# Loading x through GpSimd's DMA queue with a cast to f16, in place of SyncE's queue and casts on ScalarE

One core of one Trainium2 chip. The metric is the device time of one execution in microseconds (us), the median of several. The medians are of all runs of a kernel.

## The reference

```python
def setup_inputs():
    batch, m, k, n = 16, 512, 1024, 768      # all float32
    return {"x": randn(batch, m, k), "weight": randn(k, n), "sub_value": randn(batch, m, n)}

def reference(x, weight, sub_value):
    return (np.matmul(x, weight) - sub_value).astype(np.float32)
```

8192 rows of x in 64 row tiles of 128; 33.55 MB of x and 3.15 MB of weight are read, 25.17 MB of sub_value read and 25.17 MB of output written.

## The kernel before

Every transfer is issued by SyncE, one after another, in a sequence set by hand (x, w = weight, s = sub_value, o = output; first tile or chunk, number). x lands as f32 in 16 slots; sub_value and output share 32 slots, and each subtraction is done in place. ScalarE casts a tile of x to f16; TensorE transposes it (f16 pairs taken as f32) into PSUM, where TensorE's results go; ScalarE copies it out; 16 matmuls follow; VectorE subtracts. Seven pairs of tiles are transposed by VectorE instead.

```python
NX, NSO = 16, 32
TRANSFERS = [
    ('x', 0, 1), ('w', 0, 1), ('x', 1, 1), ('w', 1, 1), ('x', 2, 1), ('w', 2, 1),
    ('w', 3, 1), ('x', 3, 2), ('s', 0, 1), ('x', 5, 3), ('s', 1, 3), ('x', 8, 3),
    ('s', 4, 4), ('x', 11, 5), ('s', 8, 8), ('x', 16, 8), ('x', 24, 3), ('s', 16, 8),
    ('x', 27, 5), ('o', 0, 8), ('s', 24, 8), ('x', 32, 8), ('s', 32, 8), ('o', 8, 8),
    ('x', 40, 8), ('s', 40, 8), ('x', 48, 8), ('o', 16, 8), ('o', 24, 8), ('s', 48, 8),
    ('x', 56, 8), ('s', 56, 8), ('o', 32, 8), ('o', 40, 8), ('o', 48, 8), ('o', 56, 4),
    ('o', 60, 2), ('o', 62, 1), ('o', 63, 1),
]
# ... issue(): issues from the head of the list, and stops where the entry's buffer isn't free yet
#   ('x': the tile NX before has been cast, 's': the tile NSO before has been stored, 'o': subtracted)
def cast(mi):
    ...
    keep(nc.scalar.copy(out=x16_t[mi], in_=x_ring[:, mi % NX]))   # f16 <- f32
    issue()
# ... main loop, per tile: matmuls(mi), between them the transposes of tile mi + 2; cast of tile mi + 4
def finish(mi):
    o = so_ring[:, mi % NSO].rearrange("p (h n) -> p h n", h=2)
    keep(nc.vector.tensor_tensor(out=o, in0=po_t.pop(mi)[:, :, :NS], in1=o, op=subtract))
    issue()
```

## Time and profile before

| | before |
|---|---|
| time, median | 211.16 us (210.99 to 211.29) |
| span of the profiled run | 209.4 us |
| TensorE busy | 198.4 us, 95% |
| DMA engines busy (queue 1) | 97.7%, 87 MB |
| ScalarE busy | 112.6 us, 54% |

Two resources are full at once, so anything that makes either of them stand still for a while is paid for in full. The lines and how to read them are in the prediction.

### The profile page before, as it was taken

The page shows a single profiled execution, that of the slowest core. Times are in us where ns is not written, and L with a number is a line of the kernel's source. Part 1 is how long each engine was busy: PE and PEld are TensorE (multiplying, and loading weights), DVE is VectorE, ACT ScalarE, POOL GpSimd, SP SyncE. Part 2 cuts the span into 40 slices and gives each one's busy share as a digit, 9 for nine tenths or more (in the row PEclk, how much of TensorE's full clock was granted, in tenths as well). Part 3 has the DMA queues.
Part 4 walks back from the last instruction along what each step waited for, and adds up shares of the span by engine and source line. Part 5 has one row for each costly group of instructions (what it writes and reads, how often), then busy time and mean ns, then how long its engine had stood idle before and what let it go on. Part 6 is the DMA issues. An engine that isn't in the chain of part 4 may idle for free.

```text
span 209.4 us, 2967 instructions
## 1 busy us (share of the span) xinstructions
PE 198.4 (95%) x1249; PEld 130.4 (62%) x1249; DVE 114.1 (54%) x186; ACT 112.6 (54%) x115; POOL 0.7 (0%) x6
## 2 busy tenths in 40 slices
PE   7998789999979999999999999999999999999990
PEld 2464467676656576676666666667666766766660
DVE  0342044206149849929946965992994795332231
ACT  3555565675396183655727629355573760765410
POOL 1000000000000000000000000000000000000000
PEclk9999999999999999999999999999999999999999
DMA  6999999999999999999999999999999999999994
GB/s 221 420 426 424 424 438 439 433 443 426 391 455 415 442 427 423 454 413 432 435 421 449 423 413 444 451 418 421 418 441 440 423 437 418 426 446 427 415 383 167
DMA packets 5629, 87.22 MB, mean 417 GB/s; under 512 B 624, under 2 KB 624, under 8 KB 2032
## 3 DMA queue, kind: packets, MB, share of 16 engines
q1 hardware_dynamic: 5616, 87.03, 97.7%
q8 instruction: 10, 0.16, 0.3%
q14 instruction: 3, 0.02, 0.0%
HBM read 61.87 MB, written 25.17 MB: 416 GB/s over the span
## 4 chain that ended last, share of the span: by engine, by line
PE 68%; DMA 20%; ACT 4%; DVE 3%; SPq 1%; issue 1%
PE psum_o L177 60%; DMA x_ring<-in_x_dram 20%; PE psum_t L144 8%; ACT x_tile L135 2%; DVE xtp_tile L165 2%; ACT xt_tile L151 1%; DVE so_ring L189 1%; SPq L110 1%; SPq L122 1%; ACT x16p_tile L132 0%
## 5 line engine op out<-in xcount | busy, mean ns | idle before, releaser
L177 PE MATMUL psum_o<-w_sb,xt_tile 128*128 128x384 f16 x800 | 145.7, 326 | 1.7 <-ACT xt_tile L151 1.1
L177 PEld LDWEIGHTS <-xt_tile 128*128 128x128 f16 x800 | 78.2, 98 | 41.5 <-ACT xt_tile L151 1.9
L189 DVE TENSOR_TENSOR so_ring<-psum_o,so_ring 128x768 f32<-128x768 f32 x64 | 60.7, 957 | 61.2 <-PE psum_o L177 41.1
L151 ACT COPY xt_tile<-psum_t 128x1024 f16<-128x1024 f16 x50 | 50.6, 1012 | 75.7 <-PE psum_t L144 74.9
L165 DVE STREAM_TRANSPOSE xtp_tile<-x16p_tile 32x256 f32<-32x256 f32 x112 | 48.8, 436 | 18.9 <-ACT x16p_tile L132 17.2
L144 PE MATMUL psum_t<-ident,x_tile 128*128 128x128 f32 x200 | 52.5, 275 | 2.8 <-ACT x_tile L135 2.4
L135 ACT CAST x_tile<-x_ring 128x1024 f16<-128x1024 f32 x50 | 51.6, 1049 | 5.5 <-DMA x_ring<-in_x_dram 5.5
L177 PE MATMUL psum_o<-w_sb,xtp_tile 128*128 128x384 f16 x224 | 42.9, 326 | 0.3 <-DVE xtp_tile L165 0.3
L144 PEld LDWEIGHTS psum_t<-ident,x_tile 128*128 128x128 f32 x200 | 27.8, 142 | 16.8 <-ACT x_tile L135 4.7
L177 PEld LDWEIGHTS <-xtp_tile 128*128 128x128 f16 x224 | 21.8, 98 | 10.4 <-DVE xtp_tile L165 0.7
L132 ACT CAST x16p_tile<-x_ring 128x1024 f16<-128x1024 f32 x14 | 14.6, 1046 | 5.8 <-DMA x_ring<-in_x_dram 4.7
L205 PE MATMUL psum_o<-idle_x,idle_w 128*128 128x512 f16 x25 | 8.8, 508 | 1.3 <-DVE idle_x L200 1.3
L112 DVE CAST w_sb<-so_ring 128x768 f16<-128x768 f32 x8 | 4.1, 556 | 10.5 <-DMA so_ring<-in_weight_dram 10.5
L205 PEld LDWEIGHTS <-idle_w 128*128 128x128 f16 x25 | 3.0, 120 | 5.0 <-issue 3.2
L135 ACT ACT_TABLE_LOAD x1 | 1.3, 1283 | 0.7 <-PEq L277 0.7
L199 DVE MEMSET idle_w<- 128x64 uint32 x1 | 0.1, 112 | 0.8 <-PEq L277 0.8
masks.py:199 POOL TENSOR_SCALAR_AFFINE_SELECT ident<-ident 128x128 f32<-128x128 f32 x1 | 0.3, 292 | 0.1
L200 DVE MEMSET idle_x<- 128x256 uint32 x1 | 0.3, 272 | 0.0
masks.py:197 POOL MEMSET ident<- 128x128 f32 x1 | 0.2, 205 | 0.3 <-POOLq L277 0.3
L277 POOL MEMSET const-bfloat16-1.0<- 128x1 bf16 x1 | 0.1, 101 | 0.0
L277 POOL MEMSET const-uint8-127<- 128x1 uint8 x1 | 0.1, 101 | 0.0
L277 POOL MEMSET const-float32-0.0<- 128x1 f32 x1 | 0.1, 98 | 0.2 <-issue 0.2
(1 smaller groups left out, 0.1 us busy)
## 6 DMA issues: line engine op xcount, KB each, us to landing
so_ring<-in_sub_value_dram SPq DMA_DIRECT2D x7, 3072.0 KB, 24.2
out_dram<-so_ring SPq DMA_DIRECT2D x7, 3072.0 KB, 31.2
x_ring<-in_x_dram SPq DMA_DIRECT2D x5, 4096.0 KB, 22.3
x_ring<-in_x_dram SPq DMA_DIRECT2D x2, 2560.0 KB, 23.3
x_ring<-in_x_dram SPq DMA_DIRECT2D x3, 1536.0 KB, 19.8
so_ring<-in_weight_dram SPq DMA_DIRECT2D x4, 768.0 KB, 8.7
x_ring<-in_x_dram SPq DMA_DIRECT2D x3, 512.0 KB, 6.2
so_ring<-in_sub_value_dram SPq DMA_DIRECT2D x1, 1536.0 KB, 22.2
```

The costliest lines, as they stand in the source:

```text
L110: keep(nc.sync.dma_start(out=st, in_=w_c[at]))
L112: keep(nc.vector.tensor_copy(out=w_sb[:, at, r], in_=st[:, r]))
L122: keep(nc.sync.dma_start(out=here, in_=there))
L132: keep(nc.scalar.copy(out=x16_t["pair", first][:, mi - first], in_=x_in))
L135: keep(nc.scalar.copy(out=x16_t[mi], in_=x_in))
L144: keep(nc.tensor.transpose(ps_t[mi].bitcast(F32)[:, c * P : (c + 1) * P], x16_t[mi].bitcast(F32)[:, c * P : (c + 1) * P], ident,))
L151: keep(nc.scalar.copy(out=xt_t[mi], in_=ps_t.pop(mi)))
L165: keep(nc.vector.transpose(xt[b * Q : (b + 1) * Q, :, a * Q : (a + 1) * Q], x16[a * Q : (a + 1) * Q, :, b * Q : (b + 1) * Q],))
L177: keep(nc.tensor.matmul(po_t[mi][:, h, :NS], xt_t[mi][:, 2 * P * c + r : 2 * P * (c + 1) : 2], w_sb[:, c, r, h * NS : (h + 1) * NS], start ...
L189: keep(nc.vector.tensor_tensor(out=o, in0=po_t.pop(mi)[:, :, :NS], in1=o, op=mybir.AluOpType.subtract))
L205: keep(nc.tensor.matmul(idle_o[:, 0], idle_w, idle_x, start=True, stop=True))
L277: nc = _bacc.Bacc("TRN2", target_bir_lowering=False, num_devices=1)
```

## The change

Intent: take the 64 casts (67 us) off ScalarE, halve the room of x in SBUF so that 32 slots fit where 16 did, and feed the transposes straight from the ring. The loads of x, which now cast, are issued by GpSimd, so x gets a list of its own:

```diff
-NX, NSO = 16, 32
+NX, NSO = 32, 32
-TRANSFERS = [ ... one sequence, above ... ]
+TRANSFERS = {"pool": [
+    ('x', 0, 1), ('x', 1, 1), ('x', 2, 1), ('x', 3, 1), ('x', 4, 4), ('x', 8, 8),
+    ('x', 16, 8), ('x', 24, 8), ('x', 32, 8), ('x', 40, 8), ('x', 48, 8), ('x', 56, 8),
+], "sp": [
+    ('w', 0, 1), ('w', 1, 1), ('w', 2, 1), ('w', 3, 1), ('s', 0, 4), ('s', 4, 4),
+    ('s', 8, 8), ('o', 0, 8), ('s', 16, 8), ('o', 8, 8), ('s', 24, 8), ('o', 16, 8),
+    ('s', 32, 8), ('o', 24, 8), ('s', 40, 8), ('o', 32, 8), ('s', 48, 8), ('o', 40, 8),
+    ('s', 56, 8), ('o', 48, 8), ('o', 56, 4), ('o', 60, 2), ('o', 62, 1), ('o', 63, 1),
+]}
-    x_ring = x_pool.tile([P, NX, K], F32)
+    x_ring = x_pool.tile([P, NX, K], F16)
-            if kind == "o":
+            if kind == "x":
+                keep(nc.gpsimd.dma_start(out=here, in_=there))
+            elif kind == "o":
-    def cast(mi): ...                        # and its calls
-                    x16_t[mi].bitcast(F32)[:, c * P : (c + 1) * P],
+                    x_ring[:, mi % NX].bitcast(F32)[:, c * P : (c + 1) * P],
```

## The prediction

> **What bounds the kernel now.** I read the page first: totals, then the 40 slices.
>
> ```profile
> span 209.4 us, 2967 instructions
> PE 198.4 (95%) x1249; PEld 130.4 (62%) x1249; DVE 114.1 (54%) x186; ACT 112.6 (54%) x115; POOL 0.7 (0%) x6
> ...
> DMA  6999999999999999999999999999999999999994
> GB/s 221 420 426 424 424 438 439 433 443 426 391 455 415 442 427 423 454 413 432 435 421 449 423 413 444 451 418 421 418 441 440 423 437 418 426 446 427 415 383 167
> ...
> q1 hardware_dynamic: 5616, 87.03, 97.7%
> ```
>
> Two things are full, not one. TensorE is busy for 95% of the span and the DMA engines for 97.7%, from the second slice to the last but one. ScalarE, whose casts the change removes, is busy for 54%. The stretches give the same by stage:
>
> ```profile
> 20.00:30.00 10.00, 7.95 (x52) 5.06 (x50) 3.36 (x4) 5.88 (x7) 0.00 (x0) 1.00 1.01 422
> ...
> 40.00:60.00 20.00, 18.78 (x123) 12.70 (x121) 4.74 (x6) 12.52 (x14) 0.00 (x0) 1.00 1.01 430
> 60.00:80.00 20.00, 19.66 (x129) 13.07 (x127) 15.64 (x28) 11.89 (x13) 0.00 (x0) 1.00 0.99 425
> 80.00:100.00 20.00, 20.00 (x131) 13.48 (x130) 15.27 (x28) 10.73 (x11) 0.00 (x0) 1.00 1.01 432
> ```
>
> (Stretch, its length, busy time of PE, PEld, DVE, ACT, POOL with instruction counts, granted clock, DMA share, GB/s.) From 80 us on TensorE never rests, and the DMA is full beside it. Where the two stand to each other in the steady state: a block of 8 row tiles moves 4.19 MB of x, 3.15 MB of sub_value and 3.15 MB of output, 10.49 MB, at 430 GB/s 24.4 us. TensorE takes some 3.04 us for a tile that it transposes itself (16 matmuls in four groups of 0.65 us, four transposes of 0.11 us in the chain) and 2.6 us for one of the pair that VectorE transposes: a block of six and two takes 23.4 us. So the DMA is, by 1 us in 24, the slower of the two, and only its lead hides it. This kernel has nothing left over to repay a late start of the work.
>
> The timeline of TensorE shows when the pipeline is under way:
>
> ```profile
> 33.02 0.81 PE L177 MATMUL psum_o<-w_sb,xt_tile 128*128 128x384 f16 x4
> 33.67 0.27 PE L144 MATMUL psum_t<-ident,x_tile 128*128 128x128 f32 x1
> ```
>
> Counting four groups per tile back from the first matmul of tile 3 at 21.57, this is tile 6, with the first transpose of tile 8 after its first group. From 33.67 to the last matmul at 204.5 are 170.8 us, with TensorE idle for 1.5 of them (1.2 in 40 to 60, 0.3 in 60 to 80). The last subtraction, the last store and its semaphore take the 4.9 us from 204.5 to the end.
>
> **What the Trainium skill says.** "DMA: Bandwidth & Descriptors", section "SWDGE vs HWDGE vs iDMA": a cast in a DMA has to be issued from GpSimd, whose cores write the descriptors in software; its packets are preferably up to 4096 bytes. No run here has one yet. The same page, "Queues, rings and completion order": each DMA engine goes round-robin between queues that have work, by packet. The trace has one working queue, so doesn't test it, but 39 transfers of 128 rows and 16 completions are 39 x 144 = 5616, the packet count of q1: a hardware packet is a whole row here, 4 to 32 KB. The same page, "Where 436 GB/s comes from", puts the ceiling at the SBUF ports, 435 GB/s. The trace agrees in size (424 in 44 to 54, loads alone; 430 in 154 to 194, when only stores are issued). It also shows that loads and stores together get no more (432 in 80 to 100), so the shared limit looks like the engine's own data path, not the side that writes SBUF. "SBUF — State Buffer", section "Who interferes with whom": VectorE in a two-port mode blocks GpSimd from writing descriptors. The subtraction takes 957 ns for 768 elements, about one per 0.96 GHz cycle, so no doubled mode; only the eight weight casts (556 ns for the same 768) could do it, 4.4 us in all, at the start.
>
> **The change, part by part.**
>
> Removed: 64 casts on ScalarE, 50 x 1049 ns and 14 x 1046 ns, 67 us, which makes ScalarE's busy time about 52. Little of it is on the path:
>
> ```profile
> PEld psum_t L144 <- ACT x_tile L135: 4.7, 5, 1.8
> ...
> PE psum_t L144 <- ACT x_tile L135: 2.4, 2, 1.4
> ```
>
> TensorE and its weight loads waited for casts for 2.4 and 4.7 us, overlapping each other, and those waits end in x landing just before. I allow 1 us per tile for tiles 0 to 4, and nothing later. It is swallowed below, because data come later than that. The instructions of TensorE and VectorE keep their number, order and shape: the listing of the changed kernel differs only in line numbers and in the source tile. So TensorE needs the same 170.8 - 1.5 = 169.3 us from tile 8's first transpose to the end of its work.
>
> Not saved: DMA time. x is still 33.55 MB of f32 read from HBM. It writes half as many bytes, but since loads and stores share one limit I take a load to cost what its wider side costs. Total 87 MB at 430 GB/s, 202 us, as before.
>
> Moved, and this decides: the order. Before, one queue held a hand-made sequence: what precedes the landing of x tiles 8 to 10 is x 0 to 10 (5.77 MB), the weights (3.15) and s 0 to 3 (1.57), 10.5 MB; at 430 GB/s 24.4 us, with 2 us before the first byte 26.4, well before 33.67. After, x 8 to 15 is one transfer with one completion, and SyncE's queue has the weights and s 0 to 15 outstanding with no wait between. What moves before tile 8 is released is then x 0 to 15 (8.39), weights (3.15) and s 0 to 15 (6.29): 17.8 MB, 41.5 us, plus 2 us for the start and 1 for completion: 44.5. This hardly depends on how the packets are shared. At equal shares x's 8.39 MB take 39 us at 215 GB/s plus the 4 us of start and completion; with packets of 4 KB against rows of 6, 12 and 24 KB, s wins (SyncE's 9.4 MB done at about 32) and x 8 to 15 comes last, at the same 44. In the second case tile 4 (in a transfer of four) is late too, about 35 instead of 18, but that lies inside the same delay.
>
> So tile 8's transpose starts at 44.5 instead of 33.67, 10.8 us late. TensorE ends at 44.5 + 169.3 = 213.8, the span is 213.8 + 4.9 = 218.7, and the time adds the 1.8 us by which 211.19 exceeds 209.4: 220.5.
>
> A second term is the sharing later on. x may now run 32 tiles ahead and takes what its queue is granted, while the output and sub_value that pace the compute wait. At equal shares SyncE's 6.29 MB per block take 29 us against TensorE's 23.4, until x is all in at about 146 us; starting from a lead of some 9 us (s 16 lands at about 78, and tile 16 with the slack of three PSUM buffers needs it at 82) that makes waits of about 3 us at tile 24 and 5 us at tile 32. With 4 KB packets x gets the remainder, 8.8 us of each 23.4, 3.8 MB where 4.19 are needed; the deficit of 2 MB over five blocks is 4 tiles, which its lead covers. So 0 to 8 us, and I take 4: **224.5 us**, ratio 1.06.
>
> **The rivals.**
>
> (a) The cast halves the DMA cost of x. If the writing side of SBUF sets the rate, x 0 to 15 costs 4.19 MB's time, the sum ahead of tile 8 is 13.6 MB, 31.7 us, plus 3: 34.7. The head then costs 1 us, DMA is no longer full (163 us of 209), and TensorE is the only bound: 34.7 + 169.3 + 4.9 + 1.8 = 210.7, the same within 2%. With small packets tile 4 would still be late and it would be 214 to 217. For it: the skill's ports. Against it: mixed traffic isn't faster than one-way traffic. About one in five.
>
> (b) The cast runs below copy rate, through descriptor writing in software or the conversion itself. Each 10% on x's 78 us is nearly 8 us on a full DMA: at 1.3 times the time is 87 / 0.43 + 23 = 225 us of DMA alone, and 245 with the head; at double it is near 300. Nothing in the trace of before speaks on it; the requests are large, 0.5 to 4 MB, which speaks against a descriptor limit. About one in five.
>
> (c) The freed ScalarE and the deeper ring repair the start: tile 3 could begin a microsecond per cast earlier and later loads never wait for slots. The profile has SyncE waiting 75.2 us for casts, but the DMA was full during these waits, so they cost nothing. Less than one in ten.
>
> **Range and chances.** (a) gives 211 to 217, the main case 220 to 229 by the second term, (b) 235 up. I take 211 to 246 for eight in ten. Faster by 2% (under 207) would need TensorE to finish its 169.3 us from a tile 8 that comes by about 31, earlier than before: 4%. Same: 13%, nearly all of (a). Slower: 83%.
>
> **What would show it.** Right: the first transpose of tile 8 begins near 44, after an idle stretch of several us between 20 and 44 whose releaser is a load of x_ring; SyncE's issues of s 0 to 15 are all out by about 10 us; x's later loads run far ahead; TensorE's busy time is unchanged and its idle time 10 to 20 us more; the DMA row is full at first and loose in the last quarter. Wrong: if the bytes counted for x are halved and the rate of reads in the first 40 us exceeds 430 GB/s, (a) holds; if x's queue keeps the engines busy while it reads less than 430 GB/s, (b) holds; if VectorE's subtraction waits longest for sub_value, the second term was larger than the first.

## The result, and the profile after

**239.43 us** median (237.02 to 240.74), ratio 1.131 (95% interval 1.124 to 1.137): slower by 28 us where 13 were forecast.

The changed kernel's page, the lines that answer to those of before (the PEclk row is the granted TensorE clock in tenths):

```profile
span 237.9 us, 2904 instructions
...
PE 204.7 (86%) x1249; PEld 133.8 (56%) x1249; DVE 113.4 (48%) x186; ACT 51.9 (22%) x51; POOL 7.3 (3%) x18
...
PEclk9769956999999996599999999999999999999999
DMA  6999999999999999999999999992994399347363
GB/s 259 327 365 364 345 317 227 220 220 238 315 304 313 282 333 298 303 404 394 267 322 387 362 281 314 404 437 121 397 395 202 132 395 394 140 201 331 132 257 139
...
q1 hardware_dynamic: 3456, 53.48, 54.0%
q0 software_dynamic: 1728, 16.78, 33.5%
```

TensorE is now idle for 33 us (237.9 less 204.7), where it was idle for 11, and its busy time itself is 6.3 us longer: after each stop in the row of slices PEclk dips. The DMA row is full for three quarters and loose at the end. The bytes counted fell to 70 MB because x counts as written; its 16.78 MB took 33.5% of 237.9 us, 79.7 us, the time that 33.55 MB take at 421 GB/s. So the cast saved no DMA time. A stretch with x alone in flight shows it directly (columns: stretch, length, busy time of PE, PEld, DVE, ACT, POOL, granted clock, DMA share, GB/s):

```profile
40.00:50.00 10.00, 10.00 (x68) 6.98 (x66) 2.88 (x3) 3.04 (x3) 0.53 (x1) 1.00 1.00 213
60.00:80.00 20.00, 20.00 (x133) 13.79 (x132) 12.58 (x23) 6.65 (x7) 0.53 (x1) 1.00 1.00 304
80.00:100.00 20.00, 10.77 (x55) 6.40 (x54) 4.74 (x8) 1.01 (x1) 0.00 (x0) 0.77 1.01 309
140.00:160.00 20.00, 15.42 (x99) 9.97 (x98) 11.62 (x20) 3.15 (x4) 0.00 (x0) 1.00 1.00 361
160.00:238.00 78.00, 73.70 (x477) 49.39 (x475) 43.08 (x69) 18.22 (x18) 0.00 (x0) 1.00 0.61 251
```

From 40 to 50 us 213 GB/s are written at a DMA share of 1.00, which is 426 GB/s read; the kernel before moves f32 at 431 in the same stretch. From 160 on the DMA is only 61% busy: what x had taken early, it no longer needs.

The timeline of TensorE (start, duration; in brackets the idle time before it, and what ended it) shows the head:

```profile
35.55 1.12 PE L134 MATMUL psum_t<-ident,x_ring 128*128 128x128 f32 x4 [8.66 <-DMA x_ring<-in_x_dram]
...
47.82 0.27 PE L134 MATMUL psum_t<-ident,x_ring 128*128 128x128 f32 x1
```

The first line is tile 4's transposes, released by x after 8.66 us; the second is the first transpose of tile 8, at 47.82 where it was at 33.67. And the timeline of VectorE, subtractions only, shows what came later:

```profile
94.15 2.69 DVE L184 TENSOR_TENSOR so_ring<-psum_o,so_ring 128x768 f32<-128x768 f32 x3 [13.74 <-DMA so_ring<-in_sub_value_dram]
...
118.50 0.96 DVE L184 TENSOR_TENSOR so_ring<-psum_o,so_ring 128x768 f32<-128x768 f32 x1 [4.94 <-DMA so_ring<-in_sub_value_dram]
...
146.38 0.96 DVE L184 TENSOR_TENSOR so_ring<-psum_o,so_ring 128x768 f32<-128x768 f32 x1 [7.71 <-DMA so_ring<-in_sub_value_dram]
...
233.74 0.96 DVE L184 TENSOR_TENSOR so_ring<-psum_o,so_ring 128x768 f32<-128x768 f32 x1 [1.64 <-PE psum_o L172]
```

Three subtractions (the first at tile 16, the others at the start of a later block of sub_value) waited for sub_value for 26.4 us together; the last line is the last subtraction, at 233.74 where it was at 204.49 in the kernel before:

```profile
204.49 0.96 DVE L189 TENSOR_TENSOR so_ring<-psum_o,so_ring 128x768 f32<-128x768 f32 x1 [1.64 <-PE psum_o L177]
```

The kernel gives TensorE three PSUM buffers for results, so a late subtraction stops it:

```profile
85.01 0.81 PE L172 MATMUL psum_o<-w_sb,xtp_tile 128*128 128x384 f16 x4
...
95.16 1.44 PE L172 MATMUL psum_o<-w_sb,xtp_tile 128*128 128x384 f16 x4 [9.23 <-DVE so_ring L184]
```

It stood still for 9.23 us, and ran its next four matmuls in 1.44 us instead of 0.81. SyncE's queue (start, duration of the issue) shows which transfers the subtraction waited for:

```profile
3.08 1.60 SPq L125 DMA_DIRECT2D so_ring<-in_sub_value_dram  x3
...
54.32 0.35 SPq L123 DMA_DIRECT2D out_dram<-so_ring  x1
...
54.71 0.43 SPq L125 DMA_DIRECT2D so_ring<-in_sub_value_dram  x1
...
78.61 0.34 SPq L123 DMA_DIRECT2D out_dram<-so_ring  x1
```

The first three loads of sub_value are issued by 4.7 us, as forecast. The block for tile 16 is issued at 54.71, behind the store of the first block, and is used at 94.15: those two transfers, 6.29 MB, took 39 us, 160 GB/s.

Where did the rest go? From the packet records of the trace I added up the bytes of each queue in stretches (x's written bytes doubled, since it costs what it reads; a packet that crosses the edge of a stretch is counted in part):

```
changed kernel          x, GB/s read   SyncE, GB/s   sum   x's share
 5 to  20 us                124           288        412     30%
20 to  35 us                167           259        426     39%
40 to  54 us                433             0        433    100%
60 to 100 us                245           184        429     57%
x in 4-tile transfers, 60 to 150 us (run e8)
                            171           257        428     40%
```

A transfer of several tiles moves 128 rows, one for each partition: 4 KB of x or 3 KB of sub_value or output per tile. So rows of x are 32 KB (read) from tile 8 on, and most rows of sub_value and output 24 KB: 32 / (32 + 24) = 57%. The packets of x number 1728 = 12 transfers x (128 rows + 16 completions), so a packet of this queue is a whole row as well. Between 60 and 100 us 297 rows of x and 299 of SyncE's queue were begun: while both queues have work, they are served one row for one row.

All kernels can be laid out by two marks of their traces: the first transpose of tile 8, and the last subtraction. The difference is the time from a running pipeline to the end of the compute:

| kernel | time, us | ratio | tile 8 | last subtraction | between |
|---|---|---|---|---|---|
| before | 211.16 | | 33.67 | 204.49 | 170.8 |
| after | 239.43 | 1.131 | 47.82 | 233.74 | 185.9 |
| e1 one queue | 214.31 | 1.015 | 35.93 | 204.62 | 168.7 |
| e2 x in 2-tile transfers | 224.26 | 1.062 | 49.85 | 218.54 | 168.7 |
| e3 head in one queue | 243.99 | 1.156 | 36.04 | 237.38 | 201.3 |
| e4 = e2 + e3 | 220.30 | 1.044 | 36.17 | 213.59 | 177.4 |
| e5 16 slots | 229.31 | 1.086 | 49.07 | 222.82 | 173.8 |
| e6 f32, two queues | 230.30 | 1.090 | 51.11 | 223.94 | 172.8 |
| e7 loads in one queue | 223.43 | 1.058 | 34.35 | 217.17 | 182.8 |
| e8 x in 4-tile transfers | 226.82 | 1.075 | 48.73 | 220.89 | 172.2 |
| e9 after, 36 idle matmuls | 239.97 | 1.138 | 47.55 | 233.79 | 186.2 |
| e10 e2, 36 idle matmuls | 221.61 | 1.050 | 46.20 | 214.91 | 168.7 |
| e11 f32, one queue | 213.98 | 1.013 | 34.70 | 205.32 | 170.6 |
| e12 e1, stores from 32 on SyncE | 224.20 | 1.062 | 36.00 | 217.74 | 181.7 |
| e13 e1, last 8 stores on SyncE | 212.75 | 1.009 | 35.88 | 204.57 | 168.7 |
| e14 stores put off | 230.57 | 1.093 | 53.26 | 223.65 | 170.4 |
| e15 loads to tile 31 in one queue, stores put off | 231.57 | 1.093 | 34.20 | 224.72 | 190.5 |
| e16 after, 44 idle matmuls | 240.81 | 1.140 | 46.70 | 233.83 | 187.1 |

168.7 is the floor of the second part. The changed kernel is 14.2 us late at the first mark and takes 15.1 us longer for the second part; its tail after the last subtraction is 0.7 us shorter (4.2 against 4.9), and 14.2 + 15.1 - 0.7 is the 28.5 us between the spans.

### The profile page after: what moved, and what is told of

It reads as the page before. It is cut to its first block, busy times and chain, and to the rows that moved or that the text cites. A ratio compares the mean times of both kernels' runs of the same rounds, so it can differ in the third digit from the quotient of the medians.

```text
span 237.9 us, 2904 instructions
## 1 busy us (share of the span) xinstructions
PE 204.7 (86%) x1249; PEld 133.8 (56%) x1249; DVE 113.4 (48%) x186; ACT 51.9 (22%) x51; POOL 7.3 (3%) x18
## 3 DMA queue, kind: packets, MB, share of 16 engines
q0 software_dynamic: 1728, 16.78, 33.5%
## 4 chain that ended last, share of the span: by engine, by line
PE 49%; DMA 44%; DVE 4%; POOL 1%; issue 0%; SPq 0%; POOLq 0%; DVEq 0%
PE psum_o L172 43%; DMA so_ring<-in_sub_value_dram 30%; DMA x_ring<-in_x_dram 13%; PE psum_t L134 6%; DVE so_ring L184 2%; DVE xtp_tile L157 1%; POOL x_ring L121 1%; SPq L123 0%; POOL ident masks.py:199 0%; POOL ident masks.py:197 0%; DVEq L184 0%; POOLq masks.py:199 0%; POOLq L258 0%
## 5 line engine op out<-in xcount | busy, mean ns | idle before, releaser
L172 PE MATMUL psum_o<-w_sb,xt_tile 128*128 128x384 f16 x800 | 148.0, 329 | 2.7 <-DVE so_ring L184 2.7
L172 PEld LDWEIGHTS <-xt_tile 128*128 128x128 f16 x800 | 79.1, 99 | 43.6 <-issue 4.5
L134 PE MATMUL psum_t<-ident,x_ring 128*128 128x128 f32 x200 | 54.5, 287 | 13.9 <-DMA x_ring<-in_x_dram 13.9
L172 PE MATMUL psum_o<-w_sb,xtp_tile 128*128 128x384 f16 x224 | 45.8, 340 | 11.1 <-DVE so_ring L184 9.2
L157 DVE STREAM_TRANSPOSE xtp_tile<-x_ring 32x256 f32<-32x256 f32 x112 | 48.7, 435 | 1.7
L134 PEld LDWEIGHTS psum_t<-ident,x_ring 128*128 128x128 f32 x200 | 29.0, 148 | 28.0 <-DMA x_ring<-in_x_dram 10.2
L172 PEld LDWEIGHTS <-xtp_tile 128*128 128x128 f16 x224 | 22.5, 101 | 22.5 <-issue 10.8
L200 PE MATMUL psum_o<-idle_x,idle_w 128*128 128x512 f16 x25 | 9.3, 533 | 1.3 <-DVE idle_x L195 1.3
L121 POOL DMA_DIRECT2D x_ring<-in_x_dram x12 | 6.6, 568 | 122.7 <-PE psum_t L134 100.7
```

Of the source, the lines that this page charges most:

```text
L121: keep(nc.gpsimd.dma_start(out=here, in_=there))
L134: keep(nc.tensor.transpose(ps_t[mi].bitcast(F32)[:, c * P : (c + 1) * P], x_ring[:, mi % NX].bitcast(F32)[:, c * P : (c + 1) * P], ident,))
L157: keep(nc.vector.transpose(xt[b * Q : (b + 1) * Q, :, a * Q : (a + 1) * Q], x16[a * Q : (a + 1) * Q, :, b * Q : (b + 1) * Q],))
L172: keep(nc.tensor.matmul(po_t[mi][:, h, :NS], xt_t[mi][:, 2 * P * c + r : 2 * P * (c + 1) : 2], w_sb[:, c, r, h * NS : (h + 1) * NS], start ...
L200: keep(nc.tensor.matmul(idle_o[:, 0], idle_w, idle_x, start=True, stop=True))
```

## The experiments

All sixteen gave correct results. Theory A is that the loss is in the order in which two queues without a common sequence land their data; the rivals are that the software queue or the cast is itself slow (B), that a cast costs by the bytes it writes (C), and others named as they came.

**e1: one queue, the old sequence, x still cast.** Both lists replaced by the list of the kernel before, all of it issued by GpSimd:

```diff
-TRANSFERS = {"pool": [x only], "sp": [the rest]}
+TRANSFERS = {"pool": [the 39 entries of the kernel before, in its order]}
-                keep(nc.sync.dma_start(out=..., in_=...))
+                keep(nc.gpsimd.dma_start(out=..., in_=...))
```

> All transfers go through GpSimd's queue in the sequence of the kernel before, x still cast by the DMA, 32 slots. Theory A (the loss comes from the order in which two queues without a common sequence land their data): 208 to 214 us, first transpose of tile 8 by 37 us, no wait of the subtraction for sub_value over 3 us after 60 us. Theory B (the software queue or the cast is itself slow): 225 us or more. Theory C (x's cast costs by the bytes written, so a good order gains): below 207 us.

Measured: 214.31 us, ratio 1.015. All but 3 us of the loss is gone, with the cast, the software queue and the 32 slots kept. B falls, and so does C: with a good order the kernel gains nothing over f32. From the timeline of VectorE, the second weight casts at the start, and the last subtraction:

```profile
7.54 1.03 DVE L114 CAST w_sb<-so_ring 128x768 f16<-128x768 f32 x2 [6.33 <-DMA so_ring<-in_weight_dram]
...
204.62 0.96 DVE L183 TENSOR_TENSOR so_ring<-psum_o,so_ring 128x768 f32<-128x768 f32 x1 [1.64 <-PE psum_o L171]
```

The compute ends at 204.62, within 0.2 us of the kernel before; the 3 us show after it (e13 tells where they come from). The first line serves another point. GpSimd's issues in the same run (start, duration):

```profile
7.80 0.89 POOL L124 DMA_DIRECT2D x_ring<-in_x_dram  x1 [1.33 <-DMA so_ring<-in_weight_dram]
...
9.01 0.53 POOL L124 DMA_DIRECT2D so_ring<-in_sub_value_dram  x1 [0.32 <-DMA x_ring<-in_x_dram]
```

An issue beside the weight casts of VectorE takes 0.89 us, any other 0.53 to 0.68. This is the lock that the prediction took from the Trainium skill, "SBUF — State Buffer", section "Who interferes with whom". The trace fits it, at 0.36 us for each of four issues; it does not matter here.

**e2: x in smaller rows.** The share is set by the rows, so change the rows:

```diff
-    ('x', 16, 8), ('x', 24, 8), ('x', 32, 8), ('x', 40, 8), ('x', 48, 8), ('x', 56, 8),
+    *[('x', t, 2) for t in range(16, 64, 2)],
```

> As the changed kernel, but x from tile 16 on in transfers of 2 tiles: rows of 8 KB read instead of 32 KB. Theory A with packets shared in turn (one row of each queue at a time, 32 KB against 24 KB): x's share falls from 57% to about 25% while both queues have work, the waits for sub_value at tiles 16, 24 and 32 go, and the time falls by about 14 us, to 223 to 228. The head stays late (first transpose of tile 8 near 48). Theory B: unchanged or worse for more software descriptors, 236 to 245.

Measured: 224.26, as A expected. No wait for sub_value is left in the list of waits, and TensorE does not stop once in this stretch:

```profile
60.00:100.00 40.00, 40.00 (x262) 27.23 (x260) 26.42 (x46) 11.13 (x11) 2.65 (x5) 1.00 1.01 350
```

By the packet records x's share is 26% from 60 to 80 us, and 8 / (8 + 24) is 25%. The second part is at its floor of 168.7, and the head is late as in the changed kernel (49.85).

**e3: the head in one queue.** Weights, x 0 to 15 and s 0 to 15 in GpSimd's list in the old sequence:

```diff
 "pool": [
-    ('x', 0, 1), ('x', 1, 1), ('x', 2, 1), ('x', 3, 1), ('x', 4, 4), ('x', 8, 8),
+    ('x', 0, 1), ('w', 0, 1), ('x', 1, 1), ('w', 1, 1), ('x', 2, 1), ('w', 2, 1),
+    ('w', 3, 1), ('x', 3, 2), ('s', 0, 1), ('x', 5, 3), ('s', 1, 3), ('x', 8, 3),
+    ('s', 4, 4), ('x', 11, 5), ('s', 8, 8),
     ('x', 16, 8), ...
 ], "sp": [
-    ('w', 0, 1), ..., ('s', 0, 4), ('s', 4, 4), ('s', 8, 8), ('o', 0, 8), ...
+    ('o', 0, 8), ...
```

> Weights, x 0 to 15 and s 0 to 15 in one queue (GpSimd's) in the sequence of the kernel before; x from 16 on and everything else as in the changed kernel. Theory A: the first transpose of tile 8 by 37 us instead of 48, and the later waits for sub_value stay, some 14 us: 224 to 231. Theory B: tile 8 stays later than 42 and the time above 232.

Measured: 243.99, a miss for A. The head is mended as expected (36.04, 11.8 us earlier), but the second part grew by 15.4, and the kernel is slower than without the edit. The timeline of VectorE:

```profile
82.00 2.69 DVE L184 TENSOR_TENSOR so_ring<-psum_o,so_ring 128x768 f32<-128x768 f32 x3 [6.30 <-DMA so_ring<-in_sub_value_dram]
...
116.05 0.96 DVE L184 TENSOR_TENSOR so_ring<-psum_o,so_ring 128x768 f32<-128x768 f32 x1 [17.58 <-DMA so_ring<-in_sub_value_dram]
...
150.03 0.96 DVE L184 TENSOR_TENSOR so_ring<-psum_o,so_ring 128x768 f32<-128x768 f32 x1 [13.94 <-DMA so_ring<-in_sub_value_dram]
```

The waits for sub_value are longer, 17.58 and 13.94 at the later blocks. In the changed kernel SyncE's queue is empty from 36 to 54 us, and x alone gets 433 GB/s there; in e3 the stores begin earlier and there is no such stretch, so x still has more to fetch while sub_value competes with it. By the packet records x is all in at about 150 us in both kernels. From 60 to 150 us SyncE's queue gets 51% of the bytes in the changed kernel, where x's queue stands empty from 105 to 111 and from 128 to 134 us for want of free slots, but 44% in e3, where it never stands empty. From its first store to 150 us it moves 20.3 MB in the changed kernel and 19.8 MB in e3: no more, though TensorE started 11.8 us sooner. So the two losses of my sum are not independent: time won in the head is given back. (Of TensorE's 26.6 us of stops after tile 8 in e3, 5.1 are for x, the rest for sub_value.) e3 changes the sizes of the head's transfers along with their queue and order, so how much of the 11.8 us each of these is worth is not shown.

**e4: both edits.** e3's list for the head, e2's small transfers of x after it.

> Both of the two edits before this one together. Theory A: both losses go, 209 to 215 us. Theory B: more than 225. If the two edits undo the same loss, the time stays near the better of the two.

Measured: 220.30, better than either, but 5 us over the expectation. VectorE's transposes waited 10 us for x at 67.8 us, a subtraction 3.7 us for sub_value at 100.9: once SyncE's stores begin, x's small rows get their quarter only, and with the head mended x no longer has the lead to bear it, as far as these waits show.

**e5: 16 slots of x.** A deeper ring was part of the change's idea. One line undoes it:

```diff
-NX, NSO = 32, 32
+NX, NSO = 16, 32
```

> The changed kernel with 16 slots of f16 x instead of 32. Theory A (x running ahead takes the DMA from sub_value): a shorter ring stops x from running ahead, so x's queue pauses in each block of 8 tiles and the waits for sub_value shrink; with the head still late, 222 to 230 us against 239.4. Theory E (a deeper ring helps, and the loss lies elsewhere): at or above 239.

Measured: 229.31. The shorter ring is 10 us faster than the deeper one: x must pause until its slots are read, and in the pauses sub_value gets all of the DMA (second part 173.8 instead of 185.9).

**e6: two queues without a cast.** The kernel before, f32 ring, casts on ScalarE, with the two lists of the change and x on GpSimd's queue:

```diff
-TRANSFERS = [one sequence]
+TRANSFERS = {"pool": [x only], "sp": [the rest]}      # the lists of the change
-                keep(nc.sync.dma_start(out=here, in_=there))      # for x
+                keep(nc.gpsimd.dma_start(out=here, in_=there))    # f32, no cast
```

> The kernel before (f32 ring of 16, casts on ScalarE) with the two lists of the changed kernel: x on GpSimd's queue without a cast, the rest on SyncE's. Theory A (a cast costs by its wider side, the loss is the sharing alone): within 3% of the run with 16 slots of f16, 220 to 234 us. Theory F (the cast itself costs or saves DMA time): more than 5% away from it.

Measured: 230.30, within 0.5% of e5. Splitting the queues costs the same with the cast and without it. With 16 slots it is a loss of 9% on the kernel before, of which the software queue by itself makes up 1.3 points (e11, below).

**e7: loads in one queue, stores on SyncE.** The old sequence less its stores on GpSimd's queue; the stores alone on SyncE's.

```diff
 "pool": [ ... ('x', 27, 5),
-    ('o', 0, 8), ('s', 24, 8), ('x', 32, 8), ('s', 32, 8), ('o', 8, 8), ...
+    ('s', 24, 8), ('x', 32, 8), ('s', 32, 8), ('x', 40, 8), ('s', 40, 8), ...
+], "sp": [('o', 0, 8), ('o', 8, 8), ..., ('o', 62, 1), ('o', 63, 1)]
```

> x with the cast, weights and sub_value in one queue (GpSimd's) in the sequence of the kernel before, stores alone on SyncE's. Theory A: no wait over 4 us after 60 us, 208 to 214 us, at best the kernel before's time since the DMA still moves 87 MB by its wider side. Theory C (bytes written count): below 206.

Measured: 223.43, a miss for A as I then had it. The head is at 34.35, but the second part takes 182.8. A store in a queue of its own starts as soon as its tiles are subtracted, and takes turns with loads that are wanted now (40% of the bytes from 42 to 54 us, by the packet records), while nobody waits for the store. The old sequence puts the stores off: in the kernel before the last seven stores are issued from 154 us on, after every load, and fill the DMA to the end.

**e8: x in 4-tile transfers**, a second point for the share: as e2 with `('x', t, 4) for t in range(16, 64, 4)`.

> As the run with x in transfers of 2 tiles from tile 16 on, but of 4 tiles: rows of 16 KB read against 24 KB, x's share 40%. Theory A: SyncE gets 60% of 430 GB/s, a block's 6.29 MB in 24.4 us, nearly the 23.4 of the compute: 224 to 229 us, between the 224.3 of 2 tiles and the 239.4 of 8, much nearer to the first. If the number of transfers and not the share did it, about half way, 232.

Measured: 226.82, within A's range. x's share in the packet records is 40%, which is 16 / (16 + 24). Time by the rows of x: 32 KB 239.4, 16 KB 226.8, 8 KB 224.3.

**e9 and e10: the clock.** TensorE's half clock after a stop is a part of the loss, so I kept it busy during the stop at tile 4, in the changed kernel (e9) and in e2 (e10):

```diff
+    warm = psum_t_pool.tile([P, K], F16, name="psum_t")
+    for _ in range(36):
+        keep(nc.tensor.matmul(warm.bitcast(F32), idle_w, idle_x, start=True, stop=True))
     for mi in range(HEAD + 1, HEAD + TA):
         transpose_tile(mi)
```

> The changed kernel with 36 idle matmuls (about 7.8 us) in TensorE's wait for tile 4, so that its clock stays granted in full afterwards. Theory G (the loss adds up stop by stop, so each microsecond of the head counts): 3 us faster than 239.4, 236 to 237. Theory A2 (until x is all in, the end is set by how much SyncE's queue has moved by then; time won in the head is given back to x's queue): within 1.5 us of 239.4, with sub_value tile 32 still landing near 145 us.

> The same idle matmuls in the kernel with x in transfers of 2 tiles (224.3 us), where no wait for sub_value is left: after the stop at tile 4 the next 6 us ran at half clock. Both theories: those 6 us take 3, so 220.5 to 222. If the clock was not the cause of the slow matmuls: 224.

Measured: e10 221.61, 2.7 us faster than e2. e2's timeline of TensorE (tile 4's transposes, then a group of four matmuls):

```profile
36.75 1.12 PE L134 MATMUL psum_t<-ident,x_ring 128*128 128x128 f32 x4 [9.84 <-DMA x_ring<-in_x_dram]
...
37.66 1.49 PE L172 MATMUL psum_o<-w_sb,xt_tile 128*128 128x384 f16 x4
```

and e10's:

```profile
35.49 0.63 PE L134 MATMUL psum_t<-ident,x_ring 128*128 128x128 f32 x4 [1.10 <-DMA x_ring<-in_x_dram]
...
35.96 0.81 PE L172 MATMUL psum_o<-w_sb,xt_tile 128*128 128x384 f16 x4
```

1.49 us became 0.81: the same four matmuls at half and at full clock. The Trainium skill, "TensorE: Matmul & The Clock Gate", section "What's actually happening", says that after an idle window the array runs at half rate; the trace agrees, with a granted clock of 0.53 in 35 to 40 us and 0.50 in 95 to 100 in the changed kernel.

e9 is 239.97, unchanged, but told nothing: TensorE still stood for 1.94 us before tile 4, its clock fell all the same, and tile 8 began only 0.3 us earlier. Hence **e16**, the same with 44 idle matmuls:

> As the changed kernel with 36 idle matmuls, but 44 (9.5 us), since with 36 TensorE still stood for 1.94 us before tile 4 and its clock fell all the same: the first transpose of tile 8 moved by 0.3 us only, so that run told nothing. If the clock holds this time, tile 8 begins near 45.5 instead of 47.8. Theory G (each microsecond of the head counts): 236.5 to 237.5 us. Theory A2 (time won in the head is given back to x's queue): 238.5 to 240.5.

Measured: 240.81 (239.66 to 241.49). This time the clock held:

```profile
36.51 0.60 PE L134 MATMUL psum_t<-ident,x_ring 128*128 128x128 f32 x4
...
36.94 0.81 PE L172 MATMUL psum_o<-w_sb,xt_tile 128*128 128x384 f16 x4
...
46.70 0.27 PE L134 MATMUL psum_t<-ident,x_ring 128*128 128x128 f32 x1
```

The filler ran past the landing of x by a little, so tile 8 began at 46.70, 1.1 us earlier than in the changed kernel and not 2.3. The last subtraction was at 233.83, where it was at 233.74. So the 1.1 us were given back, as e3's 11.8 were: A2 holds against G, on a small difference: the changed kernel's own runs lie between 237.0 and 240.7. (Its time is 0.3 us over the range given for A2.) Of e9's details I was wrong: in both runs sub_value made TensorE wait for longer at tile 24 (12.7 and 13.1 us of VectorE's time instead of 4.9) and not at tile 32; the sums, 25.0 and 25.3 us, are near the 26.4 of the changed kernel.

**e11: the kernel before on GpSimd's queue**, `nc.sync.dma_start` replaced by `nc.gpsimd.dma_start` everywhere, no other edit.

> The kernel before, unchanged but for every transfer issued on GpSimd's queue, without a cast in the DMA. Against the run with all on GpSimd's queue and the cast (214.3 us). Theory A: the cast neither gains nor costs, and the 3 us over the kernel before are the software queue's start and its last store: 213 to 216. If the cast in the DMA saved anything, this one is slower by over 2%: 218 or more.

Measured: 213.98, against 214.31 for e1: with the same queue and sequence, casting in the DMA and casting on ScalarE are the same. This is the change's own idea measured by itself, and it is worth nothing here, either way.

**e12: e1 with the stores from tile 32 on SyncE.**

```diff
-    ('x', 56, 8), ('s', 56, 8), ('o', 32, 8), ('o', 40, 8), ('o', 48, 8), ('o', 56, 4), ...
-]}
+    ('x', 56, 8), ('s', 56, 8),
+], "sp": [('o', 32, 8), ('o', 40, 8), ('o', 48, 8), ('o', 56, 4), ...]}
```

> As the run with all transfers on GpSimd's queue in the sequence of before, x cast, but the stores from tile 32 on are issued by SyncE. In that run the last subtraction began within 0.2 us of the kernel before's, and the 3 us were lost after it. Theory A: 210.5 to 212.5, the same as before. If SyncE's stores take DMA time from the last loads, as in the run with all stores there: 214 or more.

Measured: 224.20, a miss. SyncE's queue and the subtraction of tile 48:

```profile
136.18 82.89 SPq L124 DMA_DIRECT2D out_dram<-so_ring  x7
```

```profile
176.95 0.96 DVE L185 TENSOR_TENSOR so_ring<-psum_o,so_ring 128x768 f32<-128x768 f32 x1 [18.15 <-DMA so_ring<-in_sub_value_dram]
```

The first of these stores goes out at 136 us instead of behind the last loads, and tile 48 waits 18 us for its sub_value. It is e7's loss with one edit less.

**e13: only the last 8 stores on SyncE**, which cannot begin before the loads are done.

> All transfers on GpSimd's queue in the sequence of before, x cast, but only the stores of the last 8 tiles on SyncE, which cannot begin before the last load has landed. Theory A: the 3 us that the one-queue run lost after its last subtraction come back: 210.5 to 212.5. If they were the software queue's start instead: 213.5 to 214.5.

Measured: 212.75, ratio 1.009 (1.007 to 1.010), best of all that were tried and still not the kernel before. The packet records tell where e1's 3 us come from. About half is the software queue's last stores: the span ends 3.1 us after the last data packet in e1, and 1.6 us after it in e13 (1.3 in the kernel before). The other half is the start: in e13 the first data packet leaves at 2.84 us, in the kernel before at 1.75; the DMA is then busy for 99.8% of the time up to its last data at 209.2 us, 1.1 us later than the kernel before's 208.1.

**e14: stores put off in the changed kernel.** Shares and queues unchanged, one list reordered:

```diff
-    ('s', 8, 8), ('o', 0, 8), ('s', 16, 8), ('o', 8, 8), ('s', 24, 8), ('o', 16, 8),
-    ('s', 32, 8), ('o', 24, 8), ('s', 40, 8), ...
+    ('s', 8, 8), ('s', 16, 8), ('s', 24, 8), ('o', 0, 8), ('s', 32, 8), ('o', 8, 8),
+    ('s', 40, 8), ('o', 16, 8), ('s', 48, 8), ...
```

> The changed kernel with one edit: in SyncE's list each block of sub_value goes 16 tiles earlier against the stores (s 16 and s 24 before o 0), so that a store is put off until after the loads it would delay. Shares of the two queues as before (57 to 43). Theory A3 (it is the early stores in SyncE's 43% that make sub_value late): no wait for sub_value over 3 us after tile 8; the head as late as before or a little later, tile 8 near 50 us: 223 to 230. Theory A (the share alone): SyncE still moves too little until x is in at about 150 us, so a wait of 8 us or more at some tile after 32, and 233 to 240.

Measured: 230.57, at the upper edge of A3. Shares while both queues have work:

```profile
60.00:80.00 20.00, 20.00 (x133) 14.03 (x132) 8.66 (x12) 7.08 (x7) 0.53 (x1) 1.00 1.01 311
```

That is 311 GB/s by bytes written; by the packet records, with x counted as read, 245 of x and 185 of SyncE's: 57% still. But no subtraction waits for sub_value any more, and the second part is 170.4. What is left is the head, later than ever:

```profile
53.26 0.30 PE L133 MATMUL psum_t<-ident,x_ring 128*128 128x128 f32 x1 [4.87 <-DMA x_ring<-in_x_dram]
```

That is tile 8's first transpose, waiting for x, because sub_value up to tile 31 now runs beside x 0 to 15.

**e15: stores put off as in e14, and the loads up to tile 31 in one queue.**

```diff
 "pool": [the loads of the old sequence up to ('x', 27, 5), ('s', 24, 8)],
+         then ('x', 32, 8), ('x', 40, 8), ('x', 48, 8), ('x', 56, 8)
 "sp": [('o', 0, 8), ('s', 32, 8), ('o', 8, 8), ('s', 40, 8), ...]
```

> Loads up to x 24 to 31 and s 24 to 31 in one queue in the sequence of before, x from 32 on behind them, stores and later sub_value on SyncE with the stores put off as in the run before this one. Theory A3: head and sharing are both mended with two queues: first transpose of tile 8 by 37, 209.5 to 213.5. Theory A: above 218.

Measured: 231.57 (229.15 to 234.16), a clear miss. The head is at 34.20, but sub_value for tile 16 stands behind x 24 to 26 in GpSimd's list, and since the first store on SyncE's queue now starts at 40.70 beside them, it comes late; a subtraction waits 10 us for it, until 86 us. That is not all: TensorE stands still four times after tile 8, for 14.8 us together, 8.1 of them behind sub_value (tiles 8 and 16) and 6.7 for want of x (at 61 and 122 us), with loads and stores again in two queues. I did not find an arrangement with stores and later sub_value on SyncE's queue under 220; whether one exists is open.

## Why the prediction was wrong

**Right.** The direction; that casts on ScalarE were not on the path (e1, e11); that x costs by what it reads, so that rival (a) fell (213 written at a full DMA, e5 against e6); that the cast is no slower than a copy, so that rival (b) fell (433 GB/s); that the freed ScalarE and the deeper ring repair nothing, rival (c) (e5: the deeper ring costs 10 us); that the losses would be a late head and sub_value short behind x. The two terms had the right signs and names, but they add up to a loss of 28 us where 13 were forecast. Of the prediction's own signs, one of being wrong came true: VectorE's longest single wait, 13.7 us, was for sub_value, and the second term was the larger one. And TensorE's busy time was not unchanged but 6.3 us longer, by the clock.

**Where it failed: the sizes of both terms, and adding them.** The head was put at 10.8 us and was 14.2. The second part was put at 169.3 + 4 = 173.3 us and was 185.9, so the term of 4 measured 16.6.

The larger part is the second term, "So 0 to 8 us, and I take 4". Three things were off in its working.

- The share. The step took equal shares or 4 KB packets; the rows of the two queues are 32 and 24 KB, and the measured shares are 57 and 43% from 60 to 100 us. SyncE's 6.29 MB take 34 us at 184 GB/s, not 29. I had counted rows as packets for the hardware queue in the same text, 39 x 144, and did not carry it over to the other.
- The lead. "s 16 lands at about 78": by the packet records it landed at 93.7 and was used at 94.15, since its store ahead of it went out at 54.32 rather than the assumed 49, and the pair took 39 us. The wait was 13.7 us at tile 16, where none was forecast, and 4.9 and 7.7 after it.
- The price of a stop. A stop of TensorE costs its length and then some microseconds at half clock (four matmuls 1.44 us instead of 0.81 after the 9.23 us). TensorE's 13.8 us of stops after tile 8 (9.23, 2.75 and 1.84) leave some 2.8 us of the term, about what the clock costs: from 95.2 to 101.1 us TensorE ran at a granted clock of 0.50.

The smaller part is the step "that lies inside the same delay": tile 4 did come at 35, and the last of x 8 to 15 landed at 45.8 by the packet records, near the 44.5 worked out, but from tile 4's transposes to tile 8's there are 12.3 us of work (in e16, at full clock, 10.2: 36.51 to 46.70). The later bound is 35.55 + 12.3 = 47.8, not 44.5.

**What is deeper than a size.** I added the two terms as if independent. e3 shows that they are not, and e16 agrees: in this kernel, 11.8 and 1.1 us won at tile 8 made the end no earlier. From its first store to 150 us SyncE's queue moved 19.8 MB in e3 and 19.9 in e16, stores included, and 20.3 in the changed kernel; that this amount sets the end is argued from these numbers. Either of two edits frees sub_value: a smaller share for x (e2, e8), or stores placed behind the loads (e14). After that, and only then, the head counts in full: e2 and e10 end 168.7 us after their tile 8.

**Slips that change nothing.** The working takes 3 us for start and completion in one place and 4 in another; hardware packets are 3 to 32 KB, not 4; and loads were still in flight in 154 to 194 us (the last of x until 169), so the 430 GB/s there is mixed traffic too.

**Not settled.** Why mending the head and putting the stores off together (e15) is no faster than putting them off alone (e14): its stops are known, a better order is not. And how the head's loss divides between the order of the transfers and their sizes is open.

## What to carry to other kernels

Where the DMA is full, the order of transfers is part of the algorithm: one queue keeps it; two queues here replaced it by shares in proportion to the row sizes (57% for 32 KB against 24), and a queue that may run far ahead takes from those whose data are wanted now. Before moving a stream to a second queue, work out by rows what share each gets and what stands before the first needed tile in each list, and put stores behind the loads they would delay. The cast in the DMA saved ScalarE's time here and no DMA time (e1 against e11), so it would pay only where the engine's time is on the path.

## What the Trainium skill lacked or had wrong

- "DMA: Bandwidth & Descriptors" names casts as the software queue's, but gives no speed. Here a cast from f32 to f16 runs at copy speed counted by its wider side: 433 GB/s read and 213 to 216 written with x alone in flight, and no gain in e5 against e6 or e1 against e11.
- The same page, "SWDGE vs HWDGE vs iDMA", prefers packets of up to 4096 bytes. Here the software queue's packets were whole rows, 4 to 32 KB read (1728 = 12 x 144 packets), as the hardware queue's were.
- The same page, "Queues, rings and completion order", says round-robin by packet, which agrees, but not what follows: shares go by row size, 57% for 32 KB against 24, 40% for 16 and 26% for 8 against 24.
- The same page, "Issuing engines are not separate DMA queues", says that a second issuing engine only saves issue time. It can cost, by the order that is lost: 239.4 us in two lists against 214.3 in one.
- The same page, "Specifications", gives about 1 us to the first byte for the software queue. The first packet of x left 1.4 us after the start of its issue on idle DMA engines (e1: 1.45 to 2.84), and 4.4 us after it beside SyncE's weights (changed kernel: 1.41 to 5.81). It left between 2.8 and 2.9 us in all eight kernels whose head is in GpSimd's list alone, and between 5.5 and 6.0 in all nine with SyncE's weights beside it, e6 without a cast among them; the cause was not tried.
